# Layer 0's second context tile: V rows summed by VectorE multiply-adds instead of TensorE products, and two PSUM banks for the up-blocks of the dense loop

## The chip, the cores and the metric

The kernel runs on one core of a Trainium2 chip, as one program. The metric is device microseconds (us) of one execution, from the first to the last instruction with what lies around it; a median of several runs is quoted, and lower is better. Engines are named as the profile names them: PE is TensorE's matmul, PEld its weight load, DVE is VectorE, ACT is ScalarE, POOL is GpSimd and SP is SyncE, which here only issues DMAs.

## The reference, cut to what matters

A two-layer backbone works on 512 latent tokens and 256 context tokens of width 1024. Each layer is a mixer followed by a PEER feed-forward. For every token, PEER picks 8 heads x 16 experts out of 16384; expert e adds `gate * gelu(u_e . h) * v_e`:

```python
def block(args):
    hb, ib, gb = args
    act = jax.nn.gelu(jnp.einsum('td,tkd->tk', hb, u_tab[ib]), approximate=False) * gb
    return jnp.einsum('tk,tkd->td', act, v_tab[ib])
```

So a tile of 128 tokens needs 128 picks x 128 tokens rows of U (the dot products) and as many rows of V (the weighted sum). Everything is float32. The context tokens pass through PEER in layer 0 only.

## The kernel before, in words

**Two ways to do PEER.** Of the four latent tiles of 128 tokens, three (`ND0 = 3`) are done densely: all 16384 experts go by in 128 blocks of 128 experts, each multiplied on TensorE with the 384 tokens, with gates that are zero where an expert was not picked. The fourth latent tile and both context tiles have their picked rows gathered from DRAM by indirect DMAs that POOL issues (`gather`, L949; one gather is 128 rows of 4 KB, 512 KB).

**The gathered work comes in portions of 16 gathers.** `ups` portions (`dots`, L1052) gather rows of U and DVE multiplies and reduces them. The sum of V rows exists in two forms. `sums` (`sum_rows`, L1066): the 128 rows of one gather belong to 128 tokens, and DVE does `y = g * act + y` on [128, 1024], one instruction a gather (L1077). `downs` (`down`, L1094): expert numbers and activations are first turned so that picks lie on partitions (`turn`, L1082); the 128 rows of one gather are then one token's 128 picks, and TensorE sums them by a product with a column of activations in `Z` (L1113), two gathers at a time on the quarters of the array, into PSUM bank `yp1`, which ScalarE empties per half tile (L1117). Before this change, `sums` serve the fourth latent tile of each layer, `downs` both context tiles.

**Order of the work in `peer_` (L1180) of layer 0.** The first context tile's downs are emitted first and run beside the routing of the latent tiles. Then comes the scatter stage (`scatter_gates`, L957): DVE builds one-hot rows, ScalarE scales them, TensorE multiplies them, ScalarE copies them out, and SP stores the gates of all experts to DRAM (`gd`), in pieces of 512 bytes. Between its parts lie the up-blocks of dense blocks 0 to 11 (`NA0 = 12`, `gelus`, L1236). With `PC = (0,1,1)` (L1288), the first two of the eight portions of the second context tile are put behind the scatter of the second and third dense tile; the other six go into the dense loop.

**The dense loop (L1380).** Block i has an up part (`up_dense`, L1341; for i of 12 or more: load and split the block of U, 24 matmuls of 384 columns, L229, and a gelu on ScalarE, L1241), a multiplication by the gates on DVE (L1352), a split of the result into two parts (`ah` on ScalarE, L199, `al` on DVE, L200), and a down part (`down_dense`, L1365; load and split the V rows, 18 matmuls of 512 columns, L1374) one block later. The 22 portions (6 of the second context tile, 8 ups and 8 sums of the fourth latent tile) are due at blocks `when[n] = 16 n * 126 // 352`: 0, 5, 11, 17, 22 and 28 for the context, 34 to 74 for the ups, 80 to 120 for the sums. `issue_after` puts a portion's DVE instructions behind that block's gate product on DVE; its gathers on POOL are only held back by the ring of five buffers `g`. When the last context portion is emitted, its pool closes and the rows of the next layer's norm are loaded.

**PSUM banks of the up-blocks (L1190).** `u_tile` gives bank `yp0` alone while `self.downs` is set (layer 0 throughout, because the downs own `yp1`), and `yp0` and `yp1` in turn otherwise (layer 1).

[...]

**Who ends a context tile.** `add_out` (L1124) multiplies `t.y` by the gate row and adds the residual on DVE, with loads on SP in between. The tile `y` has one buffer, so a tile's sum cannot begin to be written before the last read of the one before it.

Of the kernel before, what the change touches and what calls it, by code (L numbers as in the profile page):

```python
# [36 lines left out]
def row_bc(ap, n, parts=128):  # L37
    """A DRAM row of n elements seen by every partition."""
    return bass.AP(tensor=ap.tensor, offset=ap.offset, ap=[[0, parts], [1, n]])


def kslab(ap, c0, n):
    """Columns c0..c0+n of a [1024, *] DRAM matrix as [128, 8, n]."""
    return ap[:, c0:c0 + n].rearrange("(k p) n -> p k n", p=128)


class Pools(ExitStack):
    """A pool, and others entered after it that end with it."""
# [13 lines left out]
class Tokens:  # L62
    """A tile of 128 tokens in a PEER layer."""


class Backbone:
# [5 lines left out]
    # ---------------------------------------------------------------- helpers  # L72
# [10 lines left out]
    def rsqrt(self, ss, n, scale):  # L83
        """1/sqrt(ss*scale + eps) for a [128, n] tile: a power, and a Newton step that leaves nothing of its error."""
# [10 lines left out]
    def mod_rows(self, P, stream, layer, part, tag=None):  # L95
        """Broadcast rows of one modulation vector (scales: 1 + scale times the norm's weight), in a place of
        their own or a weight block's."""
        name = f"row{part}{stream}"
        if tag:
            r = self.wpool.tile([128, D], F32, name=name, tag=tag)  # L100
        else:
            r = P.tile([128, D], F32, name=name, tag=name, bufs=1)
        s = 0 if stream == "x" else 1
        self.row_load = self.load(r, row_bc(self.mods[layer][s:s + 1, part * D:(part + 1) * D], D))
        return r

    def sumsq(self, xs, passing):
        """[128, len(xs)] sums of squares of [128, 1024] tiles; the squares pass through other tiles."""
# [5 lines left out]
    def prenorm(self, xs, g, s, dst, passing=None):  # L114
        """dst[i] = rmsnorm(x_i) * g + s, token-major."""
# [5 lines left out]
    def transposes(self, src, dst, c, whole=None):  # L121
        """src [128 tok, 1024] -> columns c of dst [128, 8, T] (feature on partitions), in two parts unless None,
        and whole."""
# [13 lines left out]
    def mc_tile(self):  # L137
        """A PSUM bank of a ring of its own, for what is not a projection."""
        return self.psum.tile([128, 512], F32, name="mc", tag="mc", bufs=3)
# [8 lines left out]
    def out_tiles(self, n):  # L148
        """Banks for an output projection: none of those that projections wait for."""
# [9 lines left out]
    # ---------------------------------------------------------------- constants  # L159
# [29 lines left out]
    # ---------------------------------------------------------------- exact two-part products  # L189
    def split_pair(self, pool, shape, name, bufs=1):  # L190
        """Two float32r tiles whose sum carries a float32 tile exactly."""
        return [pool.tile(shape, F32R, name=name + x, tag=name + x, bufs=bufs) for x in "hl"]

    def tokens(self):
        """The normalized latent tokens, feature on partitions, in two parts."""
# [6 lines left out]
    def weight(self, src, k, n):  # L202
        """A [128, k, n] block of weights from DRAM in two parts: lists over k of [128, n]."""
        hi, lo = [], []
# [17 lines left out]
    def mm3(self, outs, lhs, rhs, k, first=True, last=True):  # L222
        """outs[i] (+)= sum over k of lhs(k) x rhs(k, i), each given as (hi, lo): three passes."""
# [8 lines left out]
    # ---------------------------------------------------------------- adaLN  # L232
# [9 lines left out]
    def ada_group(self, layer, j, P, bufs=8, queue=None):  # L242
        """Two of the six modulation vectors: four blocks of 512 columns at once on quarters of the array. Scales
        turn into 1 + scale times the norm's weight."""
# [29 lines left out]
    def context_raw(self, cx, Q):  # L274
        """Context tokens over their root mean squares, feature on partitions."""
# [8 lines left out]
    def context_mod(self, xT, hT, Q):  # L284
        """Their modulation, its rows in ada_m turned into columns."""
# [11 lines left out]
    def hook(self, ins):  # L297
        """Other work waiting to be put between the parts of the one in hand: here behind instruction ins."""
# [9 lines left out]
    # ---------------------------------------------------------------- even mixer  # L308
    def even_consts(self, c, T):
# [19 lines left out]
        # exponents of the SSD decays as products of bf16 parts: rows of each direction are 12 of heads' numbers  # L329
        # at the keys (or heads' places) and 3 of parts of the queries' sums  # L330
# [20 lines left out]
    def conv(self, acc, src, w, rows, width):  # L351
        """acc += the outer taps of a centred 3-tap convolution of src within rows."""
# [8 lines left out]
    def step_sizes(self, hT, nt, parts, P, tend, dec, place):  # L361
        """Token-major step sizes of the SSD heads and what their sums over the chunks give."""
# [36 lines left out]
        # sums of dta to each token of a chunk, and log dt less them; with heads on partitions in three parts  # L399
# [22 lines left out]
    def even_steps(self, hT, T, P, stream):  # L422
        """What the SSD heads need of the step sizes."""
# [11 lines left out]
    def even_mixer(self, hT, T, width, steps, states, res, P, stream):  # L435
        """hT: [128, 8, T] in two parts; states: [128, 2, 1024] start states (None: zero) -> final ones.
        Adds gate * mixer to the residual tiles res."""
# [57 lines left out]
        def ssd(g, yT):  # L495
# [13 lines left out]
            # token-major x and B; what each chunk adds to the states  # L509
# [14 lines left out]
            # states at the chunk starts: con of a chunk turns into the state it leaves behind  # L524
# [17 lines left out]
            # outputs, channel-major  # L542
# [37 lines left out]
            # skip, gate, grouped norm  # L580
# [30 lines left out]
    # ---------------------------------------------------------------- odd mixer  # L611
# [22 lines left out]
    def decays(self, f, T, h, P):  # L634
        """From sigmoids (both directions, channel-major): f becomes 1 - decay; returns log decay."""
# [10 lines left out]
    def odd_mixer(self, hT, hcT, res, P):  # L646
# [20 lines left out]
        def out_proj(b, oT):  # L667
            """Pair b of heads through the output projection."""
# [11 lines left out]
        def last_out(oT):  # L680
            """The last pair's: two token tiles' first head at once; what is left, a token tile after the other."""
# [17 lines left out]
        for b in range(4):  # L699
# [29 lines left out]
            # token-major values of two heads  # L729
# [12 lines left out]
            for e in range(2):  # L742
# [8 lines left out]
                # context: the final states of both directions  # L751
# [26 lines left out]
                # latents  # L778
# [7 lines left out]
                # ed: per chunk decay to the middle (0) and over the chunk (1)  # L786
# [32 lines left out]
                for c in range(nt):  # L819
# [6 lines left out]
                    # only the quadrants (key half, query half) that the causal order reaches  # L826
# [43 lines left out]
    # ---------------------------------------------------------------- PEER  # L870
    def top16(self, src, n, vals, idx):
        """The 16 largest of src [128, n] in order, with their places."""
# [8 lines left out]
    def search(self, q, keys, c, h, st):  # L881
        """Head h of token tile c: the best 16 pairs of its 16 best first and second keys.
        Of the pairs (a, b), in the order of their places, only those that fewer than 16 others dominate can
        be among them: a = 0 with all b, a = 1..7 with b < 8, a = 8..15 with b = 0."""
# [17 lines left out]
    def resolve(self, st, h0, n):  # L902
        """From the places of the best pairs of heads h0..h0+n: expert numbers and softmax gates,
        as [token, pick, head]."""
# [10 lines left out]
        # a: the row's number less one, from place 64 on the place less 64; b: the place less that of (a, 0)  # L915
# [41 lines left out]
    def scatter_gates(self, t, s, gd, Q, bufs):  # L957
        """Gates of a token tile spread over all experts, into gd[expert group, j, token, 4]."""
# [30 lines left out]
    def new_token_tile(self, P, n, stream, res, row, picked):  # L989
        """A tile of 128 tokens: its residual (SBUF, or rows of the context in DRAM) and routing results."""  # L990
# [7 lines left out]
    def ffn_norm(self, layer, toks, h2, hT, N, whole=None, passing=None):  # L998
        """Modulated norm of token tiles into h2 tiles (None: a passing one) and, transposed, hT (the last
        tiles also into whole)."""  # L1000
# [10 lines left out]
    def queries(self, layer, h, hT, T, bufs, whole=None, pool=None):  # L1011
        """Both halves of head h's queries, feature on partitions, and the head's keys. From undivided tokens
        (whole) with undivided weights."""
# [24 lines left out]
    def routing(self, name, **kw):  # L1038
        """The pool of the routing work."""
# [12 lines left out]
    def dots(self, layer, t, h):  # L1052
        """Head h's products of the picked rows of U with the tokens of a tile."""
# [5 lines left out]
    def activate(self, t):  # L1059
        """Activations of the picks times their gates."""  # L1060
# [5 lines left out]
    def sum_rows(self, layer, t, h, S):  # L1066
        """Head h's picks' rows of V, weighted and summed with the tokens on partitions."""
# [10 lines left out]
        if h == 7:  # L1078
            for n in range(2):
                self.add_out(layer, t, n, t.y[:, n * 512:(n + 1) * 512], S)  # L1080

    def turn(self, t):  # L1082
        """Activations and expert numbers with the picks on partitions, in place of the gates and the numbers."""
# [10 lines left out]
    def down(self, layer, t, m8, S, C):  # L1094
        """Tokens m8..m8+8 of both halves of 64 tokens: their picks' rows of V, weighted and summed. The four
        quarters of the array work on two tokens' halves of the row."""
# [27 lines left out]
    def add_out(self, layer, t, n, src, S, C=None):  # L1124
        """Half n of the rows: residual += gate * src."""
# [15 lines left out]
    def context_norm(self, E, Q, cx):  # L1141
        """Tiles of the context tokens in layer 0, their norm in place of the residual, and transposed."""
# [6 lines left out]
    def context_front(self, toks, hW, first, second):  # L1149
        """Routing of the context tokens in layer 0, with two other pieces of work on the way."""  # L1150
# [15 lines left out]
    def finish(self, t, S, fw):  # L1166
        """The last norm of a token tile."""
# [5 lines left out]
    def peer(self, layer, xs, nd, ctx=(), last=False, early=None):  # L1173
        """Adds gate * peer(modulated norm) to the latent tiles xs. The last nd have all experts' rows streamed
        through the tensor engine, the others (and the context's tiles ctx, whose dots are done) have the
        picked rows gathered."""
# [3 lines left out]
    def peer_(self, layer, xs, nd, ctx, last, early, P):  # L1180
# [20 lines left out]
        def sums(t):  # L1201
            def first(t=t):
                self.activate(t)
                self.sum_rows(layer, t, 0, S)
# [398 lines left out]
```

## Time and profile before

| | |
|---|---|
| runs | 4659.65, 4670.49, 4673.75 us; median 4670.49 us |
| profiled execution | span 4673.4 us, 61146 instructions (its own time outside the span is not listed) |
| PE busy | 4315.0 us, 92% of the span |
| DVE busy | 3276.8 us, 70% |
| ACT busy | 1754.4 us, 38% |
| POOL busy | 1419.0 us, 30% |
| DMA | 1120.09 MB, mean 240 GB/s |
| layer 0's dense loop | from about 1652 us to about 2792 us of the span |
| layer 1's dense loop | ends the span |

How to read it: busy shares over the whole span mix stages with different limits, so the stages have to be looked at one by one. PE's busy time is that of modelled, overlapping matmuls: a PE at 100% has no visible gap, which is not yet the same as doing as much as it can. A row of grouped instructions gives busy time, mean duration of one, and the idle time ahead of them with what ended it.

### The profile page before, as it was taken

What the parts mean: (1) busy time and instruction counts of PE and PEld (TensorE: products, weight loads), DVE (VectorE), ACT (ScalarE), POOL (GpSimd) and SP (SyncE); (2) the same over time, 40 slices, a digit from 0 to 9 for tenths busy, and PEclk for the clock granted to TensorE, in tenths of its full rate; (3) what the DMA queues carried; (4) which work ended last, traced back from release to release, by engine and by line L of the source; (5) the groups of instructions that cost most, each with busy time, mean ns of one, the idle gap of its engine ahead of it and who ended that gap; (6) DMA issues with size and microseconds to landing.
All of it is one profiled execution on the core that took longest, in us unless ns stands there. A gap on an engine that the chain in (4) does not pass through costs nothing. (4 is left out here: it accounts for less than half of the span.)

```text
span 4673.4 us, 61146 instructions
## 1 busy us (share of the span) xinstructions
PE 4315.0 (92%) x21966; PEld 3357.5 (72%) x21966; DVE 3276.8 (70%) x6716; ACT 1754.4 (38%) x3157; POOL 1419.0 (30%) x1114
## 2 busy tenths in 40 slices
PE   7989869866988999999999999999899999999998
PEld 4666635543534756688889988888767779888997
DVE  4556886886676733387888885666896657878887
ACT  4342321321225722233333335554347533333333
POOL 0002344444444233254555530000000004445543
PEclk9999979978999999999999999999899999999999
DMA  9538778878777987788988862121226768888886
GB/s 311 173 115 281 230 232 276 269 235 268 247 246 264 310 270 268 259 316 317 330 314 329 318 231 61 53 63 62 76 87 218 227 199 294 320 326 321 331 318 223
DMA packets 489088, 1120.09 MB, mean 240 GB/s; under 512 B 39856, under 2 KB 252400, under 8 KB 488784
## 3 DMA queue, kind: packets, MB, share of 16 engines
q1 hardware_dynamic: 334416, 554.08, 35.6%
q0 software_dynamic: 154368, 562.11, 34.3%
q8 instruction: 173, 2.83, 0.2%
q14 instruction: 131, 1.07, 0.1%
HBM read 1054.18 MB, written 60.82 MB: 239 GB/s over the span
## 5 line engine op out<-in xcount | busy, mean ns | idle before, releaser
L200 DVE TENSOR_TENSOR wl<-wr,wh 128x1024 fp32r<-128x1024 f32 x404 | 493.2, 1221 | 278.8 <-ACT wh L199 266.6
L952 POOL DMA_INDIRECT g<-in_peer_u_dram,idx x256 | 377.6, 1475 | 934.3 <-DVE pre L1057 696.1
L199 ACT ACTIVATE wh<-wr 128x1024 fp32r<-128x1024 f32 x404 | 426.4, 1057 | 567.4 <-DMA wr<-in_peer_uT_dram 197.2
L229 PE MATMUL yp<-hTh,wh 128*128 128x384 f32 x1808 | 611.4, 338 | 4.6 <-ACT a L1241 2.5
L229 PE MATMUL yp<-hTh,wl 128*128 128x384 f32 x1808 | 610.5, 338 | 0.4 <-DVE wl L200 0.4
L229 PE MATMUL yp<-hTl,wh 128*128 128x384 f32 x1808 | 608.8, 337 | 0.0
L952 POOL DMA_INDIRECT g<-in_peer_v_dram,idx x256 | 396.4, 1548 | 372.8 <-DVE y L1077 301.7
L952 POOL DMA_INDIRECT g<-in_peer_v_dram,idxc x256 | 290.2, 1133 | 508.0 <-PE yp L1113 450.2
L1057 DVE CUSTOM_DVE_ANT_0 g<-g,cx 128x1024 f32<-128x1024 f32 x256 | 312.7, 1223 | 146.2 <-DMA g<-in_peer_u_dram,idxc 144.2
L952 POOL DMA_INDIRECT g<-in_peer_u_dram,idxc x256 | 292.3, 1142 | 386.8 <-DVE prec L1057 338.9
L200 DVE TENSOR_TENSOR vl<-wr,vh 128x1024 fp32r<-128x1024 f32 x256 | 312.6, 1221 | 122.3 <-ACT vh L199 121.7
L229 PEld LDWEIGHTS yp<-hTh,wh 128*128 128x128 f32 x1808 | 340.8, 189 | 35.4 <-issue 16.8
L229 PE MATMUL mm<-hTh,wh 128*128 128x512 f32 (+1 forms) x864 | 343.0, 398 | 17.4 <-ACT yT L579 9.0
L229 PEld LDWEIGHTS yp<-hTl,wh 128*128 128x128 f32 x1808 | 340.4, 188 | 20.7 <-issue 11.7
L229 PEld LDWEIGHTS yp<-hTh,wl 128*128 128x128 f32 x1808 | 340.4, 188 | 12.9 <-issue 10.1
L1057 DVE CUSTOM_DVE_ANT_0 g<-g,h 128x1024 f32<-128x1024 f32 x256 | 305.0, 1220 | 60.1 <-DMA g<-in_peer_u_dram,idx 59.7
L229 PE MATMUL mm<-hTh,wl 128*128 128x512 f32 (+1 forms) x864 | 340.9, 397 | 2.7 <-DVE wl L200 2.6
L199 ACT ACTIVATE vh<-wr 128x1024 fp32r<-128x1024 f32 x256 | 270.3, 1056 | 192.3 <-PE mc L1374 104.2
L229 PE MATMUL mm<-hTl,wh 128*128 128x512 f32 (+1 forms) x864 | 339.6, 394 | 0.2 <-DVE hTl L200 0.2
L1077 DVE SCALAR_TENSOR_TENSOR y<-g,pre,y 128x1024 f32<-128x1024 f32 x254 | 325.3, 1281 | 14.9 <-DMA g<-in_peer_v_dram,idx 13.4
L199 ACT ACTIVATE ah<-a 128x384 fp32r<-128x384 f32 x256 | 133.7, 522 | 533.8 <-DVE a L1352 428.6
L1352 DVE TENSOR_TENSOR a<-a,gt 128x384 f32<-128x384 f32 x256 | 214.8, 842 | 153.1 <-ACT a L1241 71.3
(460 smaller groups left out, 9512.3 us busy)
## 6 DMA issues: line engine op xcount, KB each, us to landing
wr<-in_peer_v_dram SPq DMA_DIRECT2D x256, 512.0 KB
wr<-in_peer_uT_dram SPq DMA_DIRECT2D x226, 512.0 KB
gd<-stage SPq DMA_DIRECT2D x24, 2048.0 KB
gt<-gd SPq DMA_DIRECT2D x64, 768.0 KB
wr<-in_ev_w_in_dram SPq DMA_DIRECT2D x80, 512.0 KB
adaw<-in_ada_w_dram SPq DMA_DIRECT2D x48, 512.0 KB
adaw<-in_ada_w_dram POOLq DMA_DIRECT2D x48, 512.0 KB
wr<-in_peer_wq_dram SPq DMA_DIRECT2D x40, 512.0 KB
```

What stands on the lines that cost most here:

```text
L199: self.nc.scalar.activation(hi, src, AF.Copy)
L200: self.nc.vector.tensor_sub(lo, src, hi.bitcast(F32))
L229: mm(o, a, rhs(kk, i)[b], start=first and kk == 0 and n == 0, stop=last and kk == k - 1 and n == 2)
L952: self.nc.gpsimd.indirect_dma_start(out=g, out_offset=None, in_=table, in_offset=bass.IndirectOffsetOnAxis(ap=idx, axis=0), element_offset ...
L1057: self.nc.vector.tensor_tensor_reduce(g, g, t.h2, 1.0, 0.0, OP.mult, OP.add, s["pre"][:, k, h:h + 1])
L1077: nc.vector.scalar_tensor_tensor(t.y, g, a, t.y, op0=OP.mult, op1=OP.add)
L1352: self.last = nc.vector.tensor_mul(a, a, self.gt_[:, :, i % 4])
```

## The change

The second context tile's eight portions become `sums`, the two in the scatter stage among them. `sum_rows` hands the pool `C` on to `add_out`, which needs it for the context stream. `self.downs` is cleared ahead of the dense loop, so that its up-blocks of layer 0 take `yp0` and `yp1` in turn. Nothing else differs but comments.

```diff
-    def sum_rows(self, layer, t, h, S):
+    def sum_rows(self, layer, t, h, S, C=None):
...
         if h == 7:
             for n in range(2):
-                self.add_out(layer, t, n, t.y[:, n * 512:(n + 1) * 512], S)
+                self.add_out(layer, t, n, t.y[:, n * 512:(n + 1) * 512], S, C)
...
         def sums(t):
             def first(t=t):
                 self.activate(t)
-                self.sum_rows(layer, t, 0, S)
-            return [(16, first)] + [(16, lambda t=t, k=k: self.sum_rows(layer, t, k, S)) for k in range(1, 8)]
+                self.sum_rows(layer, t, 0, S, C)
+            return [(16, first)] + [(16, lambda t=t, k=k: self.sum_rows(layer, t, k, S, C)) for k in range(1, 8)]
...
             gate_rows()
-            portions += downs(ctx[1])
+            portions += sums(ctx[1])
             with self.routing(f"rt{layer}"):
...
             S = work_pools()
             gate_rows()
+        self.downs = False
+
         down_end = len(portions)
```

## Rows read from the trace of the kernel before

**Rows 1.** Stretches: length, busy us (count) by engine, PE clock, DMA share, GB/s.
```profile
1400.00:1450.00 50.00, 34.56 (x133) 8.74 (x130) 28.68 (x69) 7.84 (x21) 33.54 (x22) 0.76 0.70 235
1485.00:1651.80 166.80, 156.53 (x1005) 122.35 (x1002) 118.31 (x250) 124.08 (x330) 40.75 (x34) 1.00 0.94 299
1651.80:1733.90 82.10, 76.22 (x316) 44.57 (x317) 35.89 (x47) 23.09 (x30) 30.56 (x22) 0.98 0.83 284
1733.90:1996.70 262.80, 262.80 (x1227) 174.52 (x1226) 88.28 (x99) 68.76 (x91) 74.21 (x74) 1.00 0.77 261
1996.70:2396.00 399.30, 388.59 (x1926) 349.90 (x1925) 317.66 (x450) 139.32 (x188) 196.75 (x129) 0.99 0.89 321
2396.00:2752.00 356.00, 356.00 (x1802) 324.18 (x1801) 303.24 (x296) 129.56 (x171) 186.03 (x122) 1.00 0.89 326
```

**Rows 2.** Timeline of DVE: gate products of layer 0's blocks 0, 12, 34 and 80.
```profile
1651.79 0.84 DVE L1352 TENSOR_TENSOR a<-a,gt 128x384 f32<-128x384 f32 x1 [16.36 <-DMA gt<-gd]
...
1733.86 0.84 DVE L1352 TENSOR_TENSOR a<-a,gt 128x384 f32<-128x384 f32 x1 [4.83 <-ACT a L1241]
...
1996.71 0.84 DVE L1352 TENSOR_TENSOR a<-a,gt 128x384 f32<-128x384 f32 x1
...
2395.97 0.84 DVE L1352 TENSOR_TENSOR a<-a,gt 128x384 f32<-128x384 f32 x1 [2.00 <-ACT a L1241]
```

**Rows 3.** Timeline of PE: first matmuls of an up, a down, the next up.
```profile
2432.54 0.33 PE L229 MATMUL yp<-hTh,wh 128*128 128x384 f32 x1
...
2436.72 0.39 PE L1374 MATMUL mm<-vh,ah 128*128 128x512 f32 x1
...
2440.84 0.33 PE L229 MATMUL yp<-hTh,wh 128*128 128x384 f32 x1
```

**Rows 4.** Stretches as in Rows 1, line L1113 alone: PE, PEld, clock, DMA.
```profile
1651.80:1733.90 82.10, 22.25 (x90) 3.27 (x90) 0.98 0.83 284
1733.90:1996.70 262.80, 69.55 (x294) 10.19 (x294) 1.00 0.77 261
```

**Rows 5.** DMA view: all queues, first 1651.8 to 1996.7, then 2376 to 2752.
```profile
DMA packets 24980, 91.79 MB, mean 266 GB/s; under 512 B 2804, under 2 KB 2804, under 8 KB 24964
...
DMA packets 32703, 122.20 MB, mean 325 GB/s; under 512 B 3630, under 2 KB 3630, under 8 KB 32679
```

**Rows 6.** DVE's groups by line, 2396 to 2752.
```profile
L1077 DVE SCALAR_TENSOR_TENSOR y<-g,pre,y 128x1024 f32<-128x1024 f32 x122 | 156.4, 1282 | 7.9 <-DMA g<-in_peer_v_dram,idx 7.2
L200 DVE TENSOR_TENSOR wl<-wr,wh 128x1024 fp32r<-128x1024 f32 x43 | 52.5, 1221 | 8.7 <-ACT wh L199 8.5
L200 DVE TENSOR_TENSOR vl<-wr,vh 128x1024 fp32r<-128x1024 f32 x43 | 52.5, 1221 | 10.9 <-ACT vh L199 10.8
L1352 DVE TENSOR_TENSOR a<-a,gt 128x384 f32<-128x384 f32 x43 | 36.1, 840 | 22.5 <-ACT a L1241 22.5
L200 DVE TENSOR_TENSOR al<-a,ah 128x384 fp32r<-128x384 f32 x43 | 23.8, 553 | 4.7 <-ACT ah L199 4.7
```

**Rows 7.** POOL's groups by line, 1996.7 to 2752.
```profile
L952 POOL DMA_INDIRECT g<-in_peer_v_dram,idx x127 | 193.9, 1527 | 188.5 <-DVE y L1077 154.7 <-DVE y L1075 17.5 <-issue 4.9
```

**Rows 8.** DVE's waits, 1485 to 1651.8: total us, times, longest.
```profile
DVE oi L972 <- PE mm L982: 20.0, 14, 4.7
DVE a L1352 <- DMA gt<-gd: 16.4, 1, 16.4
```

**Rows 9.** Timeline of DVE: last read of the first context tile's y.
```profile
1534.02 0.69 DVE L1136 TENSOR_TENSOR go<-y,gr 128x512 f32<-128x512 f32 x1
```

**Rows 10.** Timeline of PE: a pair's first six records behind a gather, and in the loop.
```profile
1398.41 1.93 PE L1113 MATMUL yp<-g,Z 128*32 128x512 f32 x6 [4.15 <-DMA g<-in_peer_v_dram,idxc]
...
1779.67 1.06 PE L1113 MATMUL yp<-g,Z 128*32 128x512 f32 x6
```

**Rows 11.** PEld's waits, 1340 to 1480: total us, times, longest.
```profile
PEld yp L1113 <- DMA g<-in_peer_v_dram,idxc: 70.2, 37, 7.5
```

**Rows 12.** DVE's waits, 2396 to 2752: total us, times, longest.
```profile
DVE y L1077 <- DMA g<-in_peer_v_dram,idx: 7.2, 11, 1.5
```

More of the change, by code (lines that the diff above doesn't have):

```diff
@@ L62 @@
 class Tokens:
+    pass
 class Backbone:
```

## The prediction, made before the changed kernel was seen

> **What bounds the kernel now.** I read the stretches of layer 0's dense loop first [rows 1]. In 1733.9 to 1996.7 PE shows no gap while DVE is busy 88 of 263 us and the DMA engines 77% of the time: TensorE alone sets the pace. In 2396 to 2752, where the portions are `sums`, PE has no gap either, but DVE is busy 85% and the DMA engines 89%. The same work per portion, 16 gathers of 512 KB, goes by in both; the engine that consumes it differs.
>
> Next come the block times [rows 2]. The products of blocks 0 to 11 are done early in a bunch, because their up parts lie ready. Block 12 follows at 1733.86 and block 34 at 1996.71: 22 blocks in 262.8 us, 11.95 us each. Blocks 34 to 80, beside the `ups`, take (2395.97 - 1996.71) / 46 = 8.68 us each. TensorE's own work in a block is shown by the starts of its parts [rows 3]: 4.18 us for an up and 4.12 us for a down, 8.30 us together.
>
> The difference is L1113 [rows 4]. A pair of gathers makes 8 records. In 1733.9 to 1996.7 there are 294 of them, 36.75 pairs, and the stretch is 262.8 - 22 x 8.30 = 80.2 us longer than the blocks need: 2.18 us a pair. In the first 12 blocks 90 records are 11.25 pairs, 24.5 us; with 12 x 4.12 = 49.4 us of downs that explains 74 of the 82.1 us.
>
> **The change, part by part.**
>
> *Six portions leave TensorE in the loop.* That takes off (90 + 294) / 8 = 48 pairs x 2.18 = 105 us of the path. Left for TensorE between blocks 0 and 34 are 49.4 + 22 x 8.30 = 232 us, against 344.9 us now. Whether that much is gained depends on what is late next, so I cost the other three.
>
> *DMA.* The bytes stay: the gathers are as many and as large. Only the four 128 KB moves of `yh` into `y` in the loop go from SP's queue; `add_out`'s loads and stores stay where they are. The stretch moves 91.79 MB at a mean 266 GB/s [rows 5]. At the 325 GB/s of the sums stretch it takes 282 us, and since the engines are only 0.89 busy there, at 325 / 0.89 = 365 GB/s it takes 251 us. Both are more than TensorE's 232. So **DMA is late next**, above all in blocks 0 to 11, which have little matmul to hide it. I take a share of 0.94, which the scatter stage holds [rows 1]: 343 GB/s, 268 us, a gain of **77 us**; ends 251 (gain 94) and 282, rounded to 286 for a slow start (gain 59).
>
> *DVE.* 34 blocks of gate product, `al` and `vl` are 34 x (0.840 + 0.553 + 1.221) = 88.9 us; 22 `wl` are 26.9 us; 96 multiply-adds x 1.282 = 123.1 us [rows 6]; `add_out` some 3 us. In all 242 of 268 us, 90%. In the sums stretch DVE is 85% busy and nothing of it reaches PE, so I cost it at nothing; its cover is the 268 us that DMA needs, and without that cover it would itself bound the stretch at 242. The clears and diagonals of `Z` leave and are not credited.
>
> *POOL.* A gather beside multiply-adds takes POOL 1.527 us [rows 7], 96 of them 147 of 268 us: nothing. *ScalarE* loses an evacuation or two, off the path.
>
> *Two portions in the scatter stage.* TensorE has some 34 gathers' products there [rows 1], 16 pairs x 2.18 = 35 us less. DVE gets 32 x 1.282 = 41 us more on 118.3 us busy: 159 of 166.8. It waits now for TensorE's products, 20.0 us, and for the stored gates to come back, 16.4 us [rows 8]. The multiply-adds cannot start before the first context tile's `y` is read for the last time, at 1534.02 [rows 9], so they crowd into the last 118 us. One end is +41 us (nothing hidden), the other -10 us (TensorE's relief counts, but DMA is 0.94 busy, so no more than 6% of 166.8 can go). I take **+5 us**, near the low end, because the two waits together, 36 us, are nearly the size of the addition.
>
> *Two banks.* They spare TensorE the wait for the gelu that reads the one bank. All of PE's idle time beside the ups is 399.3 - 388.6 = 10.7 us, and beside the sums it is nothing [rows 1]; so at most 11 us and at least 0. I take **-4 us**, as most of those waits can be for other operands.
>
> *Sum.* -77 + 5 - 4 = -76 us on the profiled span of 4673.4, which is 2.9 us above the median of the runs (its own time outside the span is not given). From the median: 4670.5 - 76 = **4595 us**.
>
> [...] In blocks 0 to 11 after the change TensorE has 49.4 us of work while DMA needs about 268 - 22 x 8.5 = 81 us, so it will wait there. [...]
>
> **The rivals.**
>
> *TensorE stays the bound.* If the DMA engines keep up, the stretch is 49.4 + 22 x 8.68 = 240 us, a gain of 105, and the time 4670.5 - 105 + 5 - 4 = 4566 us. For it: parts of the bytes can be fetched ahead while TensorE is busy. Against: five gather buffers are all the room, and no long stretch of this trace reaches the 382 GB/s that 91.79 MB in 240 us wants. [...]
>
> [...]
>
> *DVE becomes the bound of the scatter stage*: +41 in place of +5, 4631 us. For it: 159 of 166.8 us busy, and its queue also feeds the one-hot rows. Against: the waits of rows 8.
>
> *DMA does not speed up.* If it keeps the 284 GB/s of the first 12 blocks, the stretch takes 323 us, a gain of 22: 4650 us. Against: every stretch with DVE consumers runs at 321 GB/s or more [rows 1].
>
> *Slower: the gather wait moves into DVE's queue.* Now a late gather holds up only L1113 and the matmuls behind it; afterwards it holds up DVE, behind which stand `al`, `vl` and `wl`, for which every down and up of TensorE waits. Where TensorE consumed gathers as fast as they came it waited 70.2 us in 37 waits, 1.9 us each [rows 11]. With 1.9 us at each of 96 multiply-adds, DVE needs 242 + 182 = 424 us in a stretch of 345: 4670.5 + 79 + 5 - 4 = 4750 us. It decides from a mean wait of (345 - 242) / 96 = 1.07 us. Against: beside the sums it is 7.2 us over 122, 0.06 us each [rows 12].
>
> *It does less than it says.* Two of the eight portions lie outside the loop, and if these cost what DVE's rival says while DMA gains little, the two nearly cancel and the time stays within 0.3%.
>
> **How the numbers follow.** 0.3%, about 14 us, is what a measurement of this kernel can tell from no change. Chances: the forecast 0.58 (its own range, from the ends of DMA, 4577 to 4613); TensorE as the bound 0.14; the clock 0.06; DVE in the scatter stage 0.08; DMA not faster 0.07; a cancellation 0.03; slower by gather waits 0.04. The range 4555 to 4640 takes in the first four and the widest bank gain on top of the lowest; outside it stay the last three, 0.14, and a few per cent of edges. Faster: 0.58 + 0.14 + 0.06 + 0.08 + 0.07 = 0.93; the same 0.03; slower 0.04.
>
> **What the profile afterwards would show.** L1113 has 512 records, not 1024, none behind about 1490 us; L1077 has 128 more. Block 34's gate product comes about 268 us behind block 0's, DMA share there is over 0.9 at about 340 GB/s, and blocks 12 to 34 are 8.3 to 8.7 us apart. Block 0's product is at 1652 to 1660 us. From block 34 on everything is as before, shifted. I am wrong if the blocks from 12 to 34 stay above 10 us (look for DVE waits of L1077 on gathers), if block 0 is later than about 1670 us (DVE in the scatter stage), or if the clock in blocks 0 to 11 is far below 0.98 and they take 95 us or more.

## The result, and the profile after

The changed kernel takes 4586.95 us, a median of four runs (4582.09 to 4590.89), against 4668.34 us for the kernel before (4659.65 to 4673.75). The ratio is 0.9819 [0.9802, 0.9837], some 81 us or 1.8% faster. The profiled execution has a span of 4589.1 us, 84.3 us less than the 4673.4 of before. The forecast was 4595 us.

The page's head and its busy times for the changed kernel come first:

```profile
span 4589.1 us, 60329 instructions
...
PE 4199.3 (92%) x21452; PEld 3358.1 (73%) x21452; DVE 3420.0 (75%) x6826; ACT 1755.9 (38%) x3155; POOL 1456.6 (32%) x1114
```

DVE has 143 us more work than before and PE 116 us less; PE's share of the span stays 92%. The stretches view says where the time went. The columns are those of [rows 1]; the first row runs from ScalarE's emptying of the first context tile's second half to block 0's gate product, the others between the gate products of blocks 0, 12, 34 and 80, as in [rows 2]:

```profile
1482.80:1658.10 175.30, 137.38 (x866) 126.57 (x866) 153.18 (x277) 125.68 (x327) 55.34 (x34) 0.93 0.90 282
1658.10:1716.80 58.70, 54.45 (x226) 44.92 (x227) 55.23 (x59) 19.76 (x27) 41.78 (x21) 0.89 0.93 340
1716.80:1901.90 185.10, 184.06 (x926) 165.79 (x925) 167.76 (x162) 64.99 (x88) 98.31 (x73) 1.00 0.95 354
1901.90:2309.30 407.40, 390.66 (x1934) 350.52 (x1933) 326.90 (x459) 143.22 (x192) 191.76 (x132) 0.99 0.90 328
```

The gate products that bound these rows are on DVE's timeline of the changed kernel:

```profile
1658.06 0.84 DVE L1353 TENSOR_TENSOR a<-a,gt 128x384 f32<-128x384 f32 x1 [12.32 <-DMA gt<-gd]
...
1716.76 0.87 DVE L1353 TENSOR_TENSOR a<-a,gt 128x384 f32<-128x384 f32 x1 [0.63 <-ACT a L1241]
...
1901.89 0.83 DVE L1353 TENSOR_TENSOR a<-a,gt 128x384 f32<-128x384 f32 x1
...
2309.33 0.84 DVE L1353 TENSOR_TENSOR a<-a,gt 128x384 f32<-128x384 f32 x1 [1.31 <-ACT a L1241]
```

Set against [rows 2], with lengths in us worked out from these times:

| part | before | after | after minus before |
|---|---|---|---|
| start to the emptying | 1485.1 | 1482.8 | -2.3 |
| scatter stage, to block 0 | 166.7 | 175.3 | +8.6 |
| blocks 0 to 12 | 82.1 | 58.7 | -23.4 |
| blocks 12 to 34 | 262.9 | 185.1 | -77.8 |
| blocks 34 to 80 | 399.3 | 407.4 | +8.1 |
| all behind block 80 | 2277.4 | 2279.8 | +2.4 |

So blocks 0 to 34 gained 101 us, and some 17 us were given back: half in the stage ahead of them, half in the stage behind them. In the stretches row of blocks 12 to 34 PE is as full as in [rows 1] (184 of 185 us), while DMA rose from 0.77 to 0.95 and DVE to 91%: three engines are nearly full, so this row alone doesn't say which one is late. Who waits for whom does. These are DVE's longest waits, its waits for gathers and the three of PE between blocks 0 and 34 (total us, times, longest):

```profile
DVE a L1353 <- ACT a L1241: 16.8, 14, 2.1
DVE a L1353 <- DMA gt<-gd: 12.3, 1, 12.3
...
PE mm L1375 <- ACT vh L199: 10.3, 1, 10.3
...
DVE y L1077 <- DMA g<-in_peer_v_dram,idxc: 2.8, 3, 1.2
...
PE mm L1375 <- DVE vl L200: 1.9, 1, 1.9
...
PE yp L229 <- DVE wl L200: 1.0, 1, 1.0
```

PE waits three times, 13.2 us in all, 12.2 of them at the very start. DVE waits 2.8 us for gathers over 94 multiply-adds. Neither a transfer nor DVE holds TensorE up once the stretch is under way.

### The profile page after: what moved, and what is told of

Same layout as the page of the kernel before. It is cut to its first block, busy times and chain, and to the rows that moved or that the text cites. A ratio compares the mean times of both kernels' runs of the same rounds, so it can differ in the third digit from the quotient of the medians.

```text
span 4589.1 us, 60329 instructions
## 1 busy us (share of the span) xinstructions
PE 4199.3 (92%) x21452; PEld 3358.1 (73%) x21452; DVE 3420.0 (75%) x6826; ACT 1755.9 (38%) x3155; POOL 1456.6 (32%) x1114
## 5 line engine op out<-in xcount | busy, mean ns | idle before, releaser
L952 POOL DMA_INDIRECT g<-in_peer_v_dram,idxc x256 | 339.1, 1325 | 392.4 <-DVE y L1077 172.9
L1077 DVE SCALAR_TENSOR_TENSOR y<-g,pre,y 128x1024 f32<-128x1024 f32 x254 | 325.1, 1280 | 13.0 <-DMA g<-in_peer_v_dram,idx 11.6
L88 POOL TENSOR_TENSOR rs_y<-rs_v,mhalf 128x1 f32<-128x1 f32 (+2 forms) x29 | 24.3, 839 | 929.6 <-DVE rs_v L87 929.5
```

Of the source, the lines that this page charges most:

```text
L88: nc.gpsimd.tensor_tensor(y, v, self.mhalf[:, :n], op=OP.pow)
L952: self.nc.gpsimd.indirect_dma_start(out=g, out_offset=None, in_=table, in_offset=bass.IndirectOffsetOnAxis(ap=idx, axis=0), element_offset ...
L1077: nc.vector.scalar_tensor_tensor(t.y, g, a, t.y, op0=OP.mult, op1=OP.add)
```

## The experiments

Every run is compared with the kernel before, timed on the same chip; its medians there were 4671.5 to 4677.5 us. The edits stand against the changed kernel unless it is said that they stand against the kernel before. "Blocks 0 to 12" and the like are lengths between gate products, as in the table.

How much such a length means is shown by the changed kernel's repeat (below). It agrees with the first trace on the scatter stage (175.3 us in both) and on blocks 12 to 34 (185.1 us in both), but it has 63.0 us instead of 58.7 us for blocks 0 to 12, 409.2 instead of 407.4 us for blocks 34 to 80, and its scatter stage starts 12 us later. Differences of that size between two traces are not read as effects.

### Do the transfers pace blocks 0 to 34? Half of the gathers left out

```diff
-            g = self.gather(self.V, layer, t.st["idx"][:, k, h:h + 1])
+            if k % 2 == 0 or t.stream == "x" or h < 2:
+                g = self.gather(self.V, layer, t.st["idx"][:, k, h:h + 1])
```

In the loop, every second multiply-add of the context tile uses the row already there; its own row is left out.

> The changed kernel with every second gather of the context portions in the loop left out (the multiply-add uses the row before it), so the sum of V rows is of half the picks, twice: 48 gathers, 25 MB, go, and the number of multiply-adds stays. If transfers deferred out of blocks 0 to 34 are what makes blocks 34 to 80 8 us longer than before, these go from 407 to 399 us or less. If transfers also set the first 12 blocks (59 us where TensorE needs 49), they go to 50 to 53 us. If VectorE sets the first 12 blocks, they stay at 57 to 59. If neither, because TensorE paces it all, nothing moves by more than 3 us. Blocks 12 to 34 cannot gain more than 2.5 us in any case (8.42 to 8.30 each).

It took 4584.54 us, 0.9805 [0.9789, 0.9821], against 0.9819 [0.9802, 0.9837] of the changed kernel: no difference that can be told. Blocks 0 to 12 and 12 to 34 in its stretches view:

```profile
1664.50:1728.50 64.00, 59.25 (x255) 49.05 (x256) 60.02 (x63) 23.46 (x30) 29.27 (x11) 0.92 0.78 267
1728.50:1911.50 183.00, 183.00 (x926) 166.52 (x925) 170.83 (x169) 65.11 (x88) 59.47 (x38) 1.00 0.78 267
```

DMA falls from 0.95 to 0.78 and from 354 to 267 GB/s, and the 22 blocks take 183.0 instead of 185.1 us. Blocks 0 to 12 took 64.0 us, 5 us more than in the changed kernel's first trace and 1 us more than in its repeat; they did not become shorter. The transfers were no bound, and a DMA share of 0.95 did not mean that TensorE waited for them.

### Does VectorE pace them? Multiply-adds on half the columns

```diff
-                nc.vector.scalar_tensor_tensor(t.y, g, a, t.y, op0=OP.mult, op1=OP.add)
+                m = 512 if t.stream == "c" and h >= 2 else D
+                nc.vector.scalar_tensor_tensor(t.y[:, :m], g[:, :m], a, t.y[:, :m], op0=OP.mult, op1=OP.add)
```

Half of each row's sum is left out for the six portions in the loop.

> The changed kernel with the context portions' multiply-adds in the loop on half the columns, so the other half of the sum is left out: all gathers stay, VectorE has 96 x 0.6 = 58 us less to do. If VectorE (94% busy there) sets the first 12 blocks, they go from 59 to 50 to 53 us; if the transfers do, they stay at 57 to 59. Blocks 34 to 80 stay at 407 us if their extra 8 us are deferred transfers, and go to 399 or less if they are multiply-adds left over.

It took 4585.24 us, 0.9824 [0.9803, 0.9844]: again the time of the changed kernel. Its stretch of blocks 12 to 34:

```profile
1714.50:1898.10 183.60, 183.60 (x926) 165.95 (x925) 130.44 (x160) 63.64 (x87) 82.96 (x73) 1.00 0.95 355
```

DVE has 37 us less to do, and the blocks take 1.5 us less. PE, without a gap, is what is left: 8.3 to 8.4 us a block, its own 8.30 by [rows 3].

### What if the multiply-adds really are late? Each done twice

```diff
                 nc.vector.scalar_tensor_tensor(t.y, g, a, t.y, op0=OP.mult, op1=OP.add)
+                if t.stream == "c" and h >= 2:
+                    nc.vector.scalar_tensor_tensor(t.y, g, a, t.y, op0=OP.mult, op1=OP.add)
```

This counts the six portions of the context twice and adds 96 multiply-adds, 123 us, to DVE. It tests the slower rival: that sums which lag hold up the splits behind them.

> The changed kernel with each multiply-add of the context portions in the loop done twice, so those rows count double in the sum: 96 x 1.28 = 123 us more for VectorE, no more gathers. If the slower rival's reckoning is right, VectorE's 242 us of work become 365, it sets blocks 0 to 34 in place of TensorE, and these take 340 to 375 us in place of 244: the change would be no gain or a loss at that price. If VectorE had hidden room, they take less than 300.

A single run took 4623.75 us, a span of 4622.0, 33 us over the changed kernel's. But the time was not lost in this stretch, blocks 0 to 34 in its stretches view:

```profile
1656.60:1899.50 242.90, 236.93 (x1157) 210.61 (x1158) 236.56 (x233) 88.88 (x118) 98.97 (x51) 0.99 0.78 272
```

242.9 us, as long as the changed kernel's 243.8, with DVE 97% busy and 51 gathers and the like issued on POOL instead of 94. The sums simply fell behind. The two lines in the tile view of `y` on DVE (ns of one: least, median, most; then first and last start in us) show how far:

```profile
L1077 DVE SCALAR_TENSOR_TENSOR y<-g,prec,y x127: 1271/1281/1333, 1518.8 to 2106.0; 128x1024 f32<-128x1024 f32 x127
L1079 DVE SCALAR_TENSOR_TENSOR y<-g,prec,y x96: 1272/1280/1333, 1661.4 to 2112.6; 128x1024 f32<-128x1024 f32 x96
```

The changed kernel's L1077 ends at 1905.4, this one at 2106.0, 200 us later. The backlog passes from portion to portion and is paid behind the last block, in the stretch where the fourth latent tile's sums must be done:

```profile
2687.10:2737.00 49.90, 8.19 (x34) 5.75 (x32) 41.37 (x45) 4.86 (x8) 26.39 (x21) 0.63 0.69 236
```

From its last block's gate product on PE does 8 us of work in 50, against 44 in the same 50 us of the changed kernel. Up to that product the run was 14 us ahead (2687.2 against 2701.2 us, most of it in blocks 34 to 80, which took 390.5 us); behind it, it lost 47 us. A DVE that is too busy does cost time here, but at the end of the loop and not beside the portions.

There is a limit to what this shows. From 1656 to 2115 us DVE stood idle for 0.9 us in all ahead of the 192 multiply-adds of the loop's six portions, so gathers were hardly ever late in this run. What a late gather ahead of the splits would do was not tested.

### The two portions in the scatter stage: moved into the loop, or halved

The first run moves them:

```diff
-NE0, PC = 3, (0,1,1)
+NE0, PC = 3, (0,0,0)
```

> The changed kernel with none of the second context tile's portions in the scatter stage: all 24 portions lie in the dense loop. If the 32 multiply-adds delay the scatter stage, block 0's gate product comes 6 to 16 us earlier than at 1658 us. If the transfers are what is short in the loop (16.8 MB more at about 340 GB/s is 49 us), blocks 0 to 80 take 20 to 50 us more and the whole is 10 to 40 us slower; if TensorE alone sets the loop's pace, the loop keeps its length and the whole is 6 to 16 us faster.

4562.65 us, 0.9762 [0.9747, 0.9777], better than the change itself. The scatter stage fell to 148.1 us:

```profile
1488.50:1636.60 148.10, 131.62 (x866) 120.71 (x866) 115.16 (x244) 121.09 (x326) 1.99 (x2) 1.00 0.75 221
```

Blocks 0 to 12, 12 to 34 and 34 to 80 took 59.8, 185.0 and 399.9 us, so the loop swallowed 32 more gathers (16.8 MB) and their multiply-adds and none of its parts grew beyond what repeats differ by. The portions that cost 27 us in the scatter stage cost nothing there. The gain of some 24 us is more than the 6 to 16 us expected. The second run keeps them and halves the columns of their sums, which leaves out half of those (`t.stream == "c" and h < 2` in the edit of the half columns above):

> The changed kernel with the multiply-adds of the two portions in the scatter stage on half the columns, so half of that part of the sum is left out; gathers stay, VectorE has 32 x 0.6 = 19 us less. From the emptying of the first context tile's second half to block 0's gate product the changed kernel takes 175 us, the kernel before 167, and the changed kernel without any portion there 148. If VectorE bounds this stage, it takes 155 to 166 us; if the transfers of the gathers beside those of the gates do, 172 to 176.

A single run took 4572.09 us and had this stage:

```profile
1472.90:1634.30 161.40, 133.96 (x866) 123.54 (x866) 136.23 (x277) 124.07 (x327) 51.64 (x34) 0.95 0.96 306
```

DVE does 17 us less and the stage is 14 us shorter, while the bytes and the DMA share stayed high (0.96). So VectorE's work bounds this stage now. The run's total says little on the stage: it entered the stage 10 us earlier than the changed kernel, and its blocks 0 to 12 took 65.4 us. A DVE wait of the changed kernel, 1482.8 to 1658.1, agrees with that:

```profile
DVE oi L972 <- PE mm L982: 0.7, 1, 0.7
```

In [rows 8] DVE waited 20.0 us for TensorE here. This wait is gone, and what DVE was given cost more than the wait.

### The two banks: one bank again, beside the changed kernel repeated

```diff
-        self.downs = False
```

> The changed kernel with bank yp0 alone for the up-blocks of layer 0, so the multiply-adds without the second bank. If the banks are worth what I took (4 us, at most 11), it takes 2 to 11 us more than the changed kernel, all of it between blocks 12 and 128 of layer 0. Rival, that the two banks matter to TensorE because nothing else lies between its up-blocks now: blocks 12 to 34 go from 8.4 us to 9 us or more each, 15 us or more in all. Second rival, that the alternation itself made blocks 34 to 80 slower (407 us against 399 before): these 46 blocks go back to 399 us or less, and the whole is no slower than the changed kernel.

> The changed kernel once more, to stand on one chip beside the next two: 4587 us, within 0.3%, against a kernel before of 4668 to 4674; ratio 0.982.

One bank took 4595.19 us, 0.9835 [0.9821, 0.9848]; the changed kernel, repeated, 4595.28 us, 0.9836 [0.9814, 0.9857]. Blocks 12 to 34 took 185.1 us in both, blocks 34 to 80 took 411.8 and 409.2. The banks gain or lose nothing that these runs can tell; the intervals leave room for about 10 us either way.

### The 8 us given back in blocks 34 to 80: the rows of the next norm put later in the text

At the end of the context's portions 3 MB of norm rows are loaded. The theory was that this burst, now at another place, makes these blocks longer. The edit puts pool end and loads eight portions later in the program's text, first alone, then with the portions moved out of the scatter stage:

```diff
-                    if j + 1 == down_end:
+                    if ctx and j + 1 == down_end + 8:
```

> The changed kernel with the 3 MB of loads for the next layer's norm (four rows and two context tiles), and the end of the context pool, put off from the last context portion to the last portion of the ups (block 74). If their burst on SP's queue, ahead of the weights and on DMA engines that are now full, makes blocks 34 to 80 longer, the wait of 5.9 us on the split weights near block 40 goes, blocks 34 to 80 take 399 us or less in place of 407 and the whole is 5 to 10 us faster than the changed kernel, unless the burst costs the same at its new place. If deferred gathers are the cause, blocks 34 to 80 stay at 404 to 408 us and the whole within 3 us.

> The changed kernel with no context portion in the scatter stage and with the late loads of the run above. If the two gains are independent: 24 us for the scatter stage and 0 to 10 us for the loads, 4553 to 4565 us. If the burst is already harmless when the context portions end at block 42 (blocks 34 to 80 took 400 us in the run without late loads), it is the same as that run, 4563 us.

Alone: 4592.75 us, 0.9834 [0.9815, 0.9854], blocks 34 to 80 at 413.0 us. With the moved portions: 4557.95 us, 0.9758 [0.9739, 0.9776], 402.1 us, the same as without the late rows.

These two runs do not test the theory, because the edit did not move the loads. Here the first of them is issued on SP, in the changed kernel and in the run with late rows alone:

```profile
1943.91 0.33 SPq L81 DMA_DIRECT2D row0c<-mods  x1
```

```profile
1937.84 0.33 SPq L81 DMA_DIRECT2D row0c<-mods  x1
```

Both are 42.0 us behind block 34's gate product (1901.89 and 1895.84). With the moved portions the loads start 125 us behind it, with and without the edit. The place in the text changed, and the loads stayed where they were.

What does move the loads is the end of the context's portions, and the lengths of blocks 34 to 80 go with it. Loads 38 to 42 us behind block 34: 407 to 413 us (six traces). Loads at block 34 or ahead of it: 399 to 404.5 us (four). Loads 125 us behind it: 400 to 402 us (three). Loads 257 us behind it, with the doubled sums: 390.5 us. This agrees with the theory but does not show it, as other work moves with the loads. One step is in the changed kernel's timelines, of ScalarE and then of PE:

```profile
1959.90 1.06 ACT L111 ACTIVATE oh<-oh 128x1024 f32<-128x1024 f32 x1 [5.40 <-DMA oh<-ctx]
...
1961.42 1.06 ACT L199 ACTIVATE wh<-wr 128x1024 fp32r<-128x1024 f32 x1 [0.37 <-DMA wr<-in_peer_uT_dram]
```

```profile
1962.53 0.69 PE L229 MATMUL yp<-hTh,wh 128*128 128x384 f32 x1 [5.92 <-ACT wh L199]
```

ScalarE stands for 5.40 us before a tile of context rows from that burst, which the next norm squares, and splits the block's weights behind it; PE waits 5.92 us for them, its longest wait in these blocks. It is not the whole: in the two runs with half columns ScalarE waits less than 2 us for that tile, and these blocks still take 409 and 412 us.

### What made the products cost 2.18 us a pair? Two kernels built on the one before

First, the kernel before with every second pair of gathers left out in the six portions of its loop; the products are all there, and take the rows of the pair before:

```diff
-            gs = [self.gather(self.V, layer, t.idxT[:, 64 * p + 32 * b + m:64 * p + 32 * b + m + 1]) for b in range(2)]
+            if m % 2 == 0 or t.picked is not True or t.rows.start == 0 or m8 < 16:
+                gs = [self.gather(self.V, layer, t.idxT[:, 64 * p + 32 * b + m:64 * p + 32 * b + m + 1]) for b in range(2)]
```

> The kernel before with every second pair of the second context tile's gathers in the loop left out (the product uses the pair before it): 48 gathers, 25 MB, go, all products on TensorE stay. If TensorE's 2.18 us a pair is what the removed products cost, blocks 0 to 34 stay at 340 to 345 us and the time within 0.3% of the kernel before. If the products waited for rows, the 345 us fall by 20 or more.

A single run took 4635.8 us; blocks 0 to 34 took 302.2 us, against 344.9. Neither theory foresaw the way it came about. Between blocks 12 and 34 the records come in 10 groups, where before they came in 62. One group of the run, and what follows it on PE:

```profile
1831.57 4.48 PE L1114 MATMUL yp<-g,Z 128*32 128x512 f32 x34
1835.98 0.45 PE L229 MATMUL yp<-hTh,wl 128*128 128x384 f32 x1
```

34 records take 4.4 us, 0.13 us each. In the kernel before a pair's 8 records came mostly as 2 and 6 (58 of its groups): by the loop's order the first gather's first product goes alone, and the rest waits for the second gather. Here are the end of one pair and the start of the next:

```profile
1779.67 1.06 PE L1113 MATMUL yp<-g,Z 128*32 128x512 f32 x6
1780.66 0.45 PE L229 MATMUL yp<-hTl,wh 128*128 128x384 f32 x1
...
1781.21 1.04 PE L1113 MATMUL yp<-g,Z 128*32 128x512 f32 x2
1782.19 0.45 PE L229 MATMUL yp<-hTh,wh 128*128 128x384 f32 x1
```

(The six records of [rows 10] are such an end of a pair, not its first six, as their heading has it.) Six records hold TensorE up for 0.99 us and two for 0.98: the price is by the group. The 80.2 us over 62 groups make 1.29 us each. If so, multiplying the late row first should make one group of each pair. The second kernel is that one, in `down` of the kernel before, for both context tiles:

```diff
-                for b in range(2):
+                for b in (1, 0):
```

> The kernel before with the products of the second gather of a pair issued before those of the first, nothing left out: all four products wait for the later gather and can go in one group of 8 records, where now 2 records and then 6 stand apart with matmuls of the dense blocks between them. If a group has one price of about 1.2 us for up to 8 records (the 80 us of blocks 12 to 34 over some 65 groups), these 22 blocks fall from 263 to 220 to 232 us and the time by 35 to 80 us, with the first context tile's. If each record has its price (0.27 us), nothing moves by more than 5 us.

It took 4583.26 us, 0.9796 [0.9775, 0.9817]: this loop order alone gains as much as the whole change. That is more than the 35 to 80 us expected; of the 93 us between the profiled spans, 33 came in blocks 12 to 34, 11 in blocks 0 to 12 and 49 ahead of them. Between blocks 12 and 34 there are now 34 groups, 32 of them of 8:

```profile
1795.87 1.06 PE L1113 MATMUL yp<-g,Z 128*32 128x512 f32 x8
1796.87 0.44 PE L229 MATMUL yp<-hTh,wh 128*128 128x384 f32 x1
```

Eight records hold TensorE up for as long as two did. The starts of the records say why. Each product is two records on one quarter of the array. PE's timeline, cut off shortly after a group's start, has four records started in a group of 8 and one in a group of 2:

```profile
1795.87 0.64 PE L1113 MATMUL yp<-g,Z 128*32 128x512 f32 x4
```

```profile
1781.21 0.62 PE L1113 MATMUL yp<-g,Z 128*32 128x512 f32 x1
```

In the group of 8 four records start within 0.03 us, one on each quarter, and the other four 0.46 us later, side by side again; in the group of 2 one record starts, and the other 0.45 us later. The group of 34 goes on in the same way, with a step of up to four records every 0.43 us. So a group costs its steps, and a product alone takes as many steps as four products side by side. The groups view for L1113 between blocks 12 and 34 has 288 records at 37.9 us:

```profile
L1113 PE MATMUL yp<-g,Z 128*32 128x512 f32 x288 | 37.9, 604 | 1.2 <-DMA g<-in_peer_v_dram,idxc 1.1
```

In [rows 4] 294 such records took 69.55 us. A pair now costs (229.6 - 22 x 8.30) / 36 = 1.31 us, where the prediction's working had 2.18.

### A version that beats both

It has the portions moved out of the scatter stage and the late rows, and for the first context tile, which stays on TensorE, the late row first.

```diff
-NE0, PC = 3, (0,1,1)
+NE0, PC = 3, (0,0,0)
...
-                for b in range(2):
+                for b in (1, 0):
...
-                    if j + 1 == down_end:
+                    if ctx and j + 1 == down_end + 8:
```

> The changed kernel with no context portion in the scatter stage, the late loads, and the first context tile's products in the order of the run above. If a group has one price, the first context tile's 512 records, in some 110 groups now, cost 40 to 60 us less, part of which waits for rows anyway: 4520 to 4555 us. If each record has its price, the same as without the new order, 4558 us.

4525.27 us (4515.85 to 4529.22), 0.9677 [0.9661, 0.9693], 3.2% under the kernel before. L1113 alone in the stretches view (PE and PEld busy, clock, DMA), for the changed kernel and then for this one, over all of its records:

```profile
1165.00:1482.90 317.90, 139.19 (x512) 18.61 (x512) 0.95 0.76 252
```

```profile
1150.00:1458.20 308.20, 85.57 (x512) 10.97 (x512) 0.84 0.80 270
```

The records' time falls by 54 us. The end of the first tile comes 25 us earlier, as that stage has other waits beside, and the scatter stage behind it takes 134 us, against 148 us without the new order. The late rows have no part in this: their loads start 125 us behind block 34 here too.

## Why the prediction was right or wrong, point by point

**The time, the sign and the range** hold: 4586.95 against 4595, within 4555 to 4640. The way to it was partly another, and that the time came within 8 us is partly luck: the loop gained 24 us more than its term said, and the other terms came out some 16 us worse than theirs.

**Six portions leave TensorE: right.** The step's 105 us were offered and 101 came. The 2.18 us a pair was a fair price. What it consists of the working did not ask; the runs show it to be mostly two groups of records at about 1.3 us each, and that is no price of TensorE's work as such: in one group the same pair cost 1.31 us.

**"DMA is late next": wrong, the failed step.** The term was -77 with ends of 59 and 94; measured are -101, just beyond the end of 94. The forecast took all 91.79 MB of [rows 5] into the new stretch and 343 GB/s as the likeliest rate. The changed kernel moved less in a faster stream, 0 to 34 in its DMA view:

```profile
DMA packets 22817, 85.56 MB, mean 351 GB/s; under 512 B 2540, under 2 KB 2540, under 8 KB 22802
```

And these bytes did not bind: with half of the context's gathers gone nothing changed. The rival in which TensorE stays the bound had the stretch at 240 us; it took 243.8 (248.1 in the repeat). That rival deserved the larger chance: its evidence was in [rows 1], where beside the sums PE had no gap at a DMA share of 0.89. A share below 1 with no wait behind it was read as a limit.

**DVE in the loop at nothing: right**, and the half columns show it. Its cover is thinner than said, 244 us and not 268, but also of another kind: with DVE's work raised by 123 us the blocks of the stretch still took their time, as the sums were put off, and the whole took 33 us more.

**The scatter stage: +5 was +8.6**, well inside its ends of -10 and +41. The place was right and the side too: DVE's wait for TensorE went, and DVE became the bound. TensorE's relief was mis-sized: 35 us by the loop's price of a pair, where its busy time in the stage fell by 19 us.

**Two banks: -4 was not seen**, within about 10 us.

**Not in the sum: +8 in blocks 34 to 80.** It offset a third of the 24 us by which DMA's term was off. Its cause stays open. "From block 34 on everything is as before, shifted" is what failed here. The second bank and the width of the sums were tried and leave it; with half of the gathers it is 404.0 us, but in that run the norm's loads also lie ahead of block 34. The burst of these loads is the candidate that fits all traces, and no run moved it alone.

**The clock: low at the start of the stretch, and not beyond it.** The stretches view of the changed kernel for the start of the loop has

```profile
1658.10:1670.00 11.90, 7.65 (x17) 5.62 (x18) 11.90 (x14) 2.99 (x5) 6.31 (x3) 0.50 0.95 345
1670.00:1716.80 46.80, 46.80 (x210) 39.31 (x210) 43.33 (x46) 16.77 (x23) 35.48 (x19) 0.98 0.93 339
```

a granted clock of 0.50 around the wait of 10.3 us, and 0.98 from 1670 on. PE's timeline shows products 0.43 us apart behind that wait, where they are 0.23 us apart at a granted clock of 1.00 (4.12 us for 18 products by [rows 3], in the last stretch of [rows 1]):

```profile
1660.46 0.80 PE L1375 MATMUL mm<-vh,ah 128*128 128x512 f32 x1 [10.29 <-ACT vh L199]
1661.05 0.63 PE L1375 MATMUL mc<-vh,ah 128*128 128x512 f32 x1
1661.48 0.63 PE L1375 MATMUL mm<-vh,ah 128*128 128x512 f32 x1
```

Blocks 0 to 12 took 58.7 us where their downs need 49.4: some 9 us for the clock of 0.50 and the waits of the start together. The blocks behind had no such wait, and over blocks 0 to 12 as a whole the clock is 0.89, so the prediction's line for the clock, 95 us or more, was far off.

**Slower by gather waits in DVE's queue: out.** The mean wait was 2.8 / 94 = 0.03 us, where 1.07 was the deciding point. The doubled sums did not stop the splits but fell behind them, with hardly a wait for gathers (0.9 us ahead of 192 multiply-adds), so what long gather waits would do remains untested.

## What to carry to other kernels

A DMA share of 0.95 was no bound here: with half of the context's gathers left out it fell to 0.78, and the 22 blocks took 183.0 us instead of 185.1. So look at the waits, or take half of the transfers away. Where small quarter-array products stand between full-array ones, count the groups and how many quarters each fills rather than the records, and let each group wait first for the operand that lands last (a pair cost 2.18 us mostly as two groups, 1.31 us mostly as one). Before a heavy side task goes to an engine, look at the stage: the same two portions cost 27 us in the scatter stage, which VectorE came to bound, and nothing in the loop, whose pace TensorE sets though VectorE is busy 91% of the time there. And when an edit is to move a load, look in the trace whether it moved.

## What was not expected of the hardware

A group of 2, of 6 or of 8 quarter-array records between full-array matmuls holds TensorE up for about 1.0 us in each case, 14 or 16 for 1.85 us and 34 for 4.4 us, so a lone product is dear and full quarters are cheap. By the records' starts most of it is steps of 0.43 us: two of them make 0.86 of the 1.0 us. Beside the steps some 0.15 us is left in such a group and 0.3 us around it (1.29 against 1.0); no run here shows what either consists of. And the DMA engines moved 354 GB/s beside a full TensorE, at a share of 0.95, more than the 325 of [rows 5].
